# Attention stage of a hybrid encoder layer: three splits queued at other places

## The chip, the cores and the metric

One core of one Trainium2 chip runs the whole program. The metric is the time of one execution in microseconds (us) on the device; lower is better. Where several executions are compared, the median is used.

## What is computed

The program is one layer of a streaming encoder on 512 tokens of width 1024 (fp32): a token mixer with three parallel branches (trailing-mean pooling, multi-head latent attention, a spatial-gating unit), each gated and merged, then a gated feed-forward block with a short causal convolution. Only the attention branch matters here. Cut to that:

```python
q  = einsum('bsr,rhd->bshd', rms_norm(cq, g_q),  w_uq)      # 8 heads, 128 plain + 64 rotary
kv = einsum('bsr,rhd->bshd', rms_norm(ckv, g_kv), w_ukv)    # 128 key + 128 value
q_rope = rope(q[..., 128:]);  k_rope = rope(kr)             # one rotary key for all heads
for i in range(4):                                          # blocks of 128 queries
    s = q_nope @ k_nope.T + q_rope @ k_rope.T               # keys up to the end of block i
    s = where(chunk(k) <= chunk(q), s * scale, -big)        # chunks of 64
    o[i] = softmax(s) @ v
```

The key projection is folded into the query side: for each head the query and key weights are multiplied once (`attention_weights`), and scores are taken against the latent `ckv` itself.

## The kernel before, in words

Matrix products that need full fp32 accuracy are made from three products of a faster type: each operand is split into a high part, a rounded copy, and a low part, the difference. A split is one instruction on ScalarE (high) and one on VectorE (low); out of PSUM it is `split_ps` (L128 to L131), for weights out of SBUF `wsplit` (L90 to L100). `mm3` (L108) issues the three products; `mm_chunk` (L113) issues 24 products over all eight blocks of the model width, as for a gate.

The attention stage is the loop over heads at L864 to L890. Iteration h does the following:

- rows 1 to 3 of head h's scores (`score_rows`, L754): products into a PSUM tile `sc`, a memset of the masked corner (L772), the row maximum (L774), the exponential on ScalarE (L781), and the division on GpSimd (L785);
- `attend(h - 1)` (L831): the products of the transposed weights with the values, into `po`, in three groups j = 0, 1, 2 that read PTh and PTl of that j;
- `project(h + 1)` (L734): six products of head h+1's folded weights with the latent queries, into `pqn`, and the split of the result;
- in iterations 0, 2 and 4, `rotary` (L659): products for the rotary queries of the next pair of heads, a multiplication by tables on VectorE and an addition on GpSimd that leaves the tile `qtA`, and `rotary_split` (L675), which splits `qtA` into two heads' `qrT` (two half-height instructions on ScalarE, two on VectorE);
- a `gate` (L385): 24 products that depend on nothing in attention, and a tanh `th` on ScalarE (L391);
- behind the gate, `attend_last(h - 1)` (L844), which adds the last two products to `po` and splits it into `o..h` and `o..l` (needed only long after the loop); `attention_weights(h + 2)` (L714), four products into `pwm`, split into `wqk..h` and `wqk..l`, which `project` of the next iteration reads;
- row 0 of head h+1's scores, and `transposes(h)` (L809): ten transposes on TensorE into three PSUM tiles `ptp`, each split into PTh (ScalarE) and PTl (VectorE), and a copy of one block into the head's `full` tile (L828).

All PSUM tiles come from one pool of eight buffers (`ps`, L63); a tile keeps its buffer until its last reader is done. The transposed weights, the `full` tiles and `qtA` and `qtB` come from a pool of eight SBUF buffers (`pt_t`, L75).

The source order isn't the order on the engines. When the program is built, a planner with a time model fills each engine's queue: of the instructions that can run it prefers those that stand earlier in the source, and it passes over those that still wait. So work of a later head may stand ahead of work of an earlier one, and the whole program is planned anew at each build. `tc.issue_after(ins)` ties what is traced inside it behind `ins` on the queue of its own engine; it adds no wait between engines. `on_tensor` (L436) uses it to keep one line of TensorE's work in the source's order.

Of the kernel before, what the change touches and what calls it, by code (L numbers as in the profile page):

```python
# [12 lines left out]
ALU = mybir.AluOpType  # L13
# [7 lines left out]
H = 8  # L21
# [30 lines left out]
def trunk(ctx: ExitStack, tc: tile.TileContext, A, out):  # L52
    nc = tc.nc
# [12 lines left out]
    def act_t(name, dt=F32R):  # L66
        return sb.tile([P, 512], dt, name=name, tag="act", bufs=48)
# [13 lines left out]
    def f(ap):  # L81
        return ap.bitcast(F32)
# [44 lines left out]

    def split_ps(src, hi, lo, col=None):  # L128
        if col is None:
            nc.scalar.copy(out=hi, in_=src)  # L130
            nc.vector.tensor_tensor(out=lo, in0=src, in1=f(hi), op=ALU.subtract)  # L131
        else:
            nc.scalar.activation(hi, src, AF.Copy, scale=col)
            nc.vector.scalar_tensor_tensor(
                out=lo, in0=src, scalar=col, in1=f(hi), op0=ALU.mult, op1=ALU.subtract
            )
# [28 lines left out]
    for t in range(TT):  # L165
        for n in range(2):
            x_load = nc.sync.dma_start(
                out=xs[t][n], in_=A["x"][t, n]
# [267 lines left out]
    def on_tensor(work, *args):  # L436
        with ExitStack() as order:
            for ins in tensor_last:
                order.enter_context(tc.issue_after(ins))
            tensor_last[:] = [work(*args).ins]  # L440
# [138 lines left out]
    for t in range(TT):  # L579
# [3 lines left out]
        src = lat[t][:, 384:448].rearrange("p (a b) -> p a b", a=2)  # L583
        for dst, tab in ((tA, cosT), (tB, sinT)):
            nc.vector.tensor_tensor(
                out=dst[:, t, :].rearrange("p (a b) -> p a b", a=2), in0=src,
                in1=tab[:, t : t + 1, :].broadcast_to([P, 2, 32]), op=ALU.mult,
# [71 lines left out]
    def rotary(p):  # L659
        pq = ps("pq")  # L660
        c = slice(p * P, (p + 1) * P)
        for k in range(2):
            wh, wl = wqr[k]
            mm3(pq, wh[:, c], wl[:, c], cT_hi[k], cT_lo[k], k == 0, k == 1)
        tA = pt_t("qtA")
        tB = pt_t("qtB")
        nc.vector.tensor_tensor(out=tA, in0=pq, in1=turns[0], op=ALU.mult)
        for j in range(4):
            o = slice(32 * j, 32 * j + 32)
            i = slice(32 * (j ^ 1), 32 * (j ^ 1) + 32)  # L670
            nc.vector.tensor_tensor(out=tB[o, :], in0=pq[i, :], in1=turns[1][o, :], op=ALU.mult)
        nc.gpsimd.tensor_tensor(out=tA, in0=tA, in1=tB, op=ALU.add)
        return tA

    def rotary_split(p, tA):  # L675
        for h in range(2):
            q = act_t(f"qrT{2 * p + h}")
            hi = slice(64 * h, 64 * h + 64)
            lo = slice(64 - 64 * h, 128 - 64 * h)
            nc.scalar.copy(out=q[hi, :], in_=tA[hi, :])  # L680
            nc.vector.tensor_tensor(out=q[lo, :], in0=tA[hi, :], in1=f(q[hi, :]), op=ALU.subtract)
            qrT.append(q)
# [31 lines left out]
    def attention_weights(h):  # L714
        raw = const.tile([P, 384], F32, name=f"wqk{h}", tag="wqk")
        with tc.issue_after(last_load[0]):
            nc.sync.dma_start(out=raw, in_=A["wqk"][h])
        pw = ps("pwm")

        def products():  # L720
            for k in range(2):
                c = slice(k * P, (k + 1) * P)
                ins = nc.tensor.matmul(pw[:, c], raw[:, c], raw[:, 256:384], start=True, stop=True)
            return ins

        on_tensor(products)
        wh = act_t(f"wqk{h}h")[:, :256]
        wl = act_t(f"wqk{h}l")[:, :256]
        split_ps(pw[:, :256], wh, wl)
        wqk[h] = wh, wl  # L730
# [23 lines left out]
    def score_rows(h, i):  # L754
        kh, kl = cT_hi[2], cT_lo[2]
        if i == 0:
            PE_[h] = []
            whole[h] = qk[h][2]
        qh, ql, full = qk[h] if i < TT - 1 else qk.pop(h)
        qs = slice(i * P, (i + 1) * P)  # L760
        nk = (i + 1) * P
        sc = ps("sc")
        if i == 0:
            on_tensor(first_scores, sc, h, full)
        else:
            with tc.issue_after(tensor_last[0]):
                nc.tensor.matmul(sc[:, :nk], qh[:, qs], kl[:, :nk], start=True, stop=False)
            nc.tensor.matmul(sc[:, :nk], ql[:, qs], kh[:, :nk], start=False, stop=False)
            nc.tensor.matmul(sc[:, :nk], qrT[h][:, qs], krL[:, :nk], start=False, stop=False)
            nc.tensor.matmul(sc[:, :nk], qrT[h][:, qs], krT[:, :nk], start=False, stop=False)  # L770
            nc.tensor.matmul(sc[:, :nk], qh[:, qs], kh[:, :nk], start=False, stop=True)
        nc.vector.memset(sc[0:64, nk - 64 : nk], MASKED)  # L772
        mx = sm.tile([P, 4], F32, name="mx", tag="mx")
        nc.vector.reduce_max(out=mx[:, 0:1], in_=sc[:, :nk], axis=AX.X, negate=True)  # L774
        if i == 1:
            pe = first_rows_of.pop(h)[:, P:]
        else:
            pe = pad_t("pe")
        if i == 0:
            first_rows_of[h] = pe  # L780
        nc.scalar.activation(  # L781
            pe[:, :nk], sc[:, :nk], AF.Exp, bias=mx[:, 0:1], scale=1.0, accum_out=mx[:, 2:3]
        )
        nc.vector.reciprocal(out=mx[:, 3:4], in_=mx[:, 2:3])  # L784
        nc.gpsimd.tensor_scalar(  # L785
            out=pe[:, :nk], in0=pe[:, :nk], scalar1=mx[:, 3:4], scalar2=0.0, op0=ALU.mult, op1=ALU.add
        )
        if h == 0:
            PE_[h].append(pe)
        elif i == 0:  # L790
            pair[h] = pe
        else:
            pr = act_t(f"pr{h}{i}")
            if i == 1:
                nc.sync.dma_start(out=f(pr)[:, : 3 * P], in_=pair.pop(h)[:, : 3 * P])
                PE_[h] += [pr, pr[:, P:]]
            else:
                nc.sync.dma_start(out=f(pr)[:, :nk], in_=pe[:, :nk])
                PE_[h].append(pr)
# [9 lines left out]
    def transposes(h):  # L809
        pes = PE_.pop(h)  # L810
        full = whole[h]
        hs = [pt_t(f"PTh{h}{j}", F32R) for j in range(3)]
        ls = [pt_t(f"PTl{h}{j}", F32R) for j in range(3)]
        for j in range(3):
            pt = ps("ptp")

            def turn():
                for i in range(j, TT):
                    ins = flip(pt[:, (i - j) * P : (i - j + 1) * P], pes[i][:, j * P : (j + 1) * P])
                if j == 2:  # L820
                    ins = flip(pt[:, 384:512], pes[3][:, 384:512])
                return ins

            on_tensor(turn)
            b = 512 - j * P
            split_ps(pt[:, :b], hs[j][:, :b], ls[j][:, :b])
            if j == 2:
                nc.scalar.copy(out=full[:, 256:384], in_=pt[:, 384:512])  # L828
        PT[h] = hs, ls

    def attend(h):  # L831
        hs, ls = PT.pop(h)
# [11 lines left out]
    def attend_last(h):  # L844
        po, v, pt = opened.pop(h)
        on_tensor(lambda: nc.tensor.matmul(po[:, 384:512], v, pt, start=False, stop=True))
        oh = act_t(f"o{h}h")
        ol = act_t(f"o{h}l")
        split_ps(po, oh, ol)
        oT_hi.append(oh)  # L850
        oT_lo.append(ol)

    th1 = []
    tensor_last.clear()
    attention_weights(0)
    rotary_split(0, rotary(0))
    th0.append(gate(0, 3, None, gate_weights[3]))
    project(0)
# [1 line left out]
    th0.append(gate(0, 4))  # L860
    values(0, (2, 3))
    attention_weights(1)
    score_rows(0, 0)
    for h in range(H):  # L864
        for i in range(1, TT):
            score_rows(h, i)
        if h:
            attend(h - 1)
        if h == 4:
            values(1)  # L870
        if h == 0:
            turned = rotary(1)
        if h + 1 < H:
            project(h + 1)
        if h in (2, 4):
            rotary_split(h // 2 + 1, rotary(h // 2 + 1))
        if len(th0) < KT:
            th0.append(gate(0, len(th0)))
        elif len(th1) < 5:
            th1.append(gate(1, len(th1)))  # L880
        with tc.issue_after(last_chunk[0]):
            if h:
                attend_last(h - 1)
            if h + 2 < H:
                attention_weights(h + 2)
        if h == 0:
            rotary_split(1, turned)
        if h + 1 < H:
            score_rows(h + 1, 0)
        transposes(h)  # L890


    ada_state = {}
# [145 lines left out]
    pool(1)  # L1039
    attend(H - 1)  # L1040
    attend_last(H - 1)
    for m in range(KT):
        if m and m + 1 < KT:
            pool(m + 1)
        merge(0, m, oT_hi, oT_lo, th0[m])
        behind_split(ada_piece, 0, m)
        if m == 6:
            behind_split(combine_weights, 0)
# [952 lines left out]
```

## Time and profile before

| what | value |
|---|---|
| median of 3 runs | 928.01 us (927.05 to 928.98) |
| the profiled execution's own time | 926.81 us |
| its span, first to last instruction | 925.1 us |
| around the span | 1.7 us |
| TensorE busy over the span | 911.8 us, 4388 products |
| VectorE, ScalarE, GpSimd busy | 669.9, 408.0, 259.0 us |
| mean granted TensorE clock | 0.997 of full |
| attention loop in the trace | about 74 to 182 us |

A row of a timeline has the start in us from the span's start, the time it took, the engine, the line, the operation, `out<-in` by the program's names with the buffer numbers left out, shapes, and in brackets how long the engine was idle before it and what ended that. PE is TensorE, PEld its weight loads, DVE VectorE, ACT ScalarE, POOL GpSimd. Product ends are modelled and overlap the next start, so starts tell more than durations. A row of windows has a stretch, its length, the busy time and number of instructions of PE, PEld, DVE, ACT and POOL, the granted clock, and the DMA engines' share and rate.

### The profile page before, as it was taken

The page shows a single profiled execution, that of the slowest core. Times are in us where ns is not written, and L with a number is a line of the kernel's source. Part 1 is how long each engine was busy: PE and PEld are TensorE (multiplying, and loading weights), DVE is VectorE, ACT ScalarE, POOL GpSimd, SP SyncE. Part 2 cuts the span into 40 slices and gives each one's busy share as a digit, 9 for nine tenths or more (in the row PEclk, how much of TensorE's full clock was granted, in tenths as well). Part 3 has the DMA queues.
Part 4 walks back from the last instruction along what each step waited for, and adds up shares of the span by engine and source line. Part 5 has one row for each costly group of instructions (what it writes and reads, how often), then busy time and mean ns, then how long its engine had stood idle before and what let it go on. Part 6 is the DMA issues. An engine that isn't in the chain of part 4 may idle for free. (4 is left out here: it accounts for less than half of the span.)

```text
span 925.1 us, 12529 instructions
## 1 busy us (share of the span) xinstructions
PE 911.8 (99%) x4388; PEld 768.5 (83%) x4388; DVE 669.9 (72%) x1094; ACT 408.0 (44%) x676; POOL 259.0 (28%) x314
## 2 busy tenths in 40 slices
PE   7999999999999999999999999999999999999996
PEld 6888888888888888888888888988888888888885
DVE  7977566447777798776475589588888766676787
ACT  5676555532333332133322346464554555455421
POOL 4621211113431154402053711032223221120304
PEclk9999999999999999999999999999999999999998
DMA  9832333245447986774476450045554553479946
GB/s 356 304 115 76 101 110 105 91 148 166 157 145 263 376 322 223 249 257 144 158 263 216 144 195 27 23 150 189 189 179 129 154 174 126 137 272 357 348 137 159
DMA packets 70959, 171.94 MB, mean 186 GB/s; under 512 B 9312, under 2 KB 12576, under 8 KB 70896
## 3 DMA queue, kind: packets, MB, share of 16 engines
q1 hardware_dynamic: 58752, 142.14, 45.6%
q0 software_dynamic: 11712, 28.51, 9.1%
q8 instruction: 34, 0.56, 0.2%
q10 hardware_dynamic: 432, 0.49, 0.1%
q14 instruction: 29, 0.24, 0.1%
HBM read 144.16 MB, written 20.78 MB: 178 GB/s over the span
## 5 line engine op out<-in xcount | busy, mean ns | idle before, releaser
L96 DVE TENSOR_TENSOR wupl<-wup,wuph 128x1024 fp32r<-128x1024 f32 x38 | 52.4, 1378 | 25.1 <-PE pzu L122 17.0
L1659 POOL TENSOR_TENSOR zc<-zc 128x512 f32<-128x512 f32 x22 | 31.2, 1420 | 130.3 <-ACT zc L1658 128.9
L95 ACT CAST wuph<-wup 128x1024 fp32r<-128x1024 f32 x38 | 40.1, 1054 | 46.4 <-PE pzu L120 31.1
L95 ACT CAST wbh<-wb 128x1024 fp32r<-128x1024 f32 x24 | 25.3, 1054 | 68.2 <-PE py L120 44.2
L96 DVE TENSOR_TENSOR wgl<-wg,wgh 128x1024 fp32r<-128x1024 f32 x22 | 28.8, 1307 | 31.6 <-PE pg L122 17.7
L1034 POOL DMA_DIRECT2D wt<-wb x44 | 24.2, 551 | 80.1 <-DVE wb L1030 75.1
L1635 ACT ACTIVATE zc<-pzu,cols 128x512 f32<-128x512 f32 x44 | 34.0, 778 | 21.0 <-PE pzu L122 16.6
L95 ACT CAST wgh<-wg 128x1024 fp32r<-128x1024 f32 x22 | 23.2, 1055 | 40.7 <-PE pg L120 29.7
L905 DVE SCALAR_TENSOR_TENSOR ada<-adar,cact,ada 128x512 f32<-128x512 f32 x42 | 40.6, 1004 | 0.5 <-DMA adar<-in_ada 0.5
L1030 DVE TENSOR_TENSOR wb<-wb,wb 128x512 f32<-128x512 f32 x44 | 35.3, 806 | 6.8 <-DMA wb<-in_wdn 6.4
L785 POOL TENSOR_SCALAR pe<-pe,mx 128x128 f32<-128x128 f32 (+3 forms) x32 | 17.0, 534 | 76.6 <-DVE mx L784 56.6
L96 DVE TENSOR_TENSOR wbl<-wb,wbh 128x1024 fp32r<-128x1024 f32 x24 | 31.1, 1297 | 9.8 <-PE pg L122 5.3
L1638 DVE SCALAR_TENSOR_TENSOR zc<-pzu,cols,zc 128x511 f32<-128x511 f32 x44 | 32.5, 742 | 4.3 <-ACT zc L1635 4.3
L1642 DVE SCALAR_TENSOR_TENSOR zc<-pzu,cols,zc 128x510 f32<-128x510 f32 x44 | 32.6, 744 | 0.7
L409 POOL TENSOR_TENSOR mg<-mg,th 128x512 f32<-128x512 f32 x16 | 28.4, 1778 | 11.6 <-DVE th L406 11.4
L986 POOL TENSOR_TENSOR asum<-apad 128x527 f32<-128x527 f32 x8 | 12.2, 1520 | 59.1 <-issue 30.0
L1699 POOL DMA_DIRECT2D z<-ys x27 | 14.5, 541 | 49.2 <-PE pd L1675 39.4
L1658 ACT ACTIVATE zc<-zc 128x512 f32<-128x512 f32 x22 | 13.9, 631 | 20.9 <-DVE zc L1642 20.9
L96 DVE TENSOR_TENSOR wal<-wa,wah 128x1024 fp32r<-128x1024 f32 x8 | 10.7, 1333 | 17.1 <-PE pg L122 9.9
L1210 POOL TENSOR_TENSOR oraw<-oraw,gtt 128x512 f32<-128x512 f32 x6 | 10.3, 1729 | 39.7 <-DMA oraw<-in_wo 37.4
L781 ACT ACTIVATE pe<-sc,mx 128x128 f32<-128x128 f32 (+3 forms) x32 | 16.9, 529 | 10.1 <-DVE mx L774 7.6
L1232 POOL TENSOR_TENSOR o<-o,gtt 128x512 f32<-128x512 f32 x10 | 17.5, 1773 | 12.6 <-DMA o<-in_wo 10.2
(1627 smaller groups left out, 3204.4 us busy)
## 6 DMA issues: line engine op xcount, KB each, us to landing
wup<-in_wup SPq DMA_DIRECT2D x44, 512.0 KB, 3.5
wb<-in_wb SPq DMA_DIRECT2D x24, 512.0 KB, 3.8
adar<-in_ada SPq DMA_DIRECT2D x48, 256.0 KB, 4.9
wg<-in_wg SPq DMA_DIRECT2D x23, 512.0 KB, 3.6
wb<-in_wdn SPq DMA_DIRECT2D x44, 256.0 KB, 5.3
wt<-wb POOLq DMA_DIRECT2D x44, 256.0 KB, 4.2
ada<-in_ada SPq DMA_DIRECT2D x32, 256.0 KB, 5.3
z<-ys POOLq DMA_DIRECT2D x27, 256.0 KB, 5.7
```

The costliest lines, as they stand in the source:

```text
L95: nc.scalar.copy(out=hi[:, :n], in_=raw[:, :n])
L96: ins = nc.vector.tensor_tensor(out=lo[:, :n], in0=raw[:, :n], in1=f(hi[:, :n]), op=ALU.subtract)
L409: nc.gpsimd.tensor_tensor(out=merged[m], in0=merged[m], in1=th, op=ALU.add)
L785: nc.gpsimd.tensor_scalar(out=pe[:, :nk], in0=pe[:, :nk], scalar1=mx[:, 3:4], scalar2=0.0, op0=ALU.mult, op1=ALU.add)
L905: nc.vector.scalar_tensor_tensor(out=acc[n], in0=src, scalar=cact[:, k : k + 1], in1=acc[n], op0=ALU.mult, op1=ALU.add,)
L1030: ins = nc.vector.tensor_tensor(out=dst, in0=x, in1=y, op=op)
L1034: nc.gpsimd.dma_start(out=dst, in_=src)
L1232: nc.gpsimd.tensor_tensor(out=halves[n], in0=halves[n], in1=gt[n], op=ALU.mult)
L1635: nc.scalar.activation(t, pz, AF.Identity, bias=cols[:, cc + 3 : cc + 4], scale=cols[:, cc + 2 : cc + 3])
L1638: nc.vector.scalar_tensor_tensor(out=t[:, 1:512], in0=pz[:, 0:511], scalar=cols[:, cc + 1 : cc + 2], in1=t[:, 1:512], op0=ALU.mult, op1=AL ...
L1642: nc.vector.scalar_tensor_tensor(out=t[:, 2:512], in0=pz[:, 0:510], scalar=cols[:, cc : cc + 1], in1=t[:, 2:512], op0=ALU.mult, op1=ALU.add,)
L1659: nc.gpsimd.tensor_tensor(out=val, in0=val, in1=gate, op=ALU.mult)
```

## The change

Three things are queued elsewhere. The split of the folded query/key weights leaves `attention_weights` and becomes `attention_weights_split`; the split of each head's output leaves `attend_last` and becomes `attended_split`. In the loop both are now traced after `transposes(h)`, and tied behind its last split (j = 2): on ScalarE behind the last PTh, on VectorE behind the last PTl. `rotary_split` is now traced one iteration after its `rotary`, after the next `project`. The first two heads' weights and the last head's output are split at once, as before.

```diff
     def split_ps(src, hi, lo, col=None):
         if col is None:
-            nc.scalar.copy(out=hi, in_=src)
-            nc.vector.tensor_tensor(out=lo, in0=src, in1=f(hi), op=ALU.subtract)
+            a = nc.scalar.copy(out=hi, in_=src)
+            b = nc.vector.tensor_tensor(out=lo, in0=src, in1=f(hi), op=ALU.subtract)
+            return a.ins, b.ins
...
         on_tensor(products)
+        wqk[h] = pw
+
+    def attention_weights_split(h):
+        pw = wqk[h]
         wh = act_t(f"wqk{h}h")[:, :256]
         wl = act_t(f"wqk{h}l")[:, :256]
         split_ps(pw[:, :256], wh, wl)
...
-            split_ps(pt[:, :b], hs[j][:, :b], ls[j][:, :b])
+            turned_split = split_ps(pt[:, :b], hs[j][:, :b], ls[j][:, :b])
             if j == 2:
                 nc.scalar.copy(out=full[:, 256:384], in_=pt[:, 384:512])
         PT[h] = hs, ls
+        return turned_split
...
         on_tensor(lambda: nc.tensor.matmul(po[:, 384:512], v, pt, start=False, stop=True))
+        opened[h] = po
+
+    def attended_split(h):
+        po = opened.pop(h)
         oh = act_t(f"o{h}h")
         ol = act_t(f"o{h}l")
         split_ps(po, oh, ol)
...
     attention_weights(0)
+    attention_weights_split(0)
...
     attention_weights(1)
+    attention_weights_split(1)
...
         if h + 1 < H:
             project(h + 1)
+        if h in (1, 3, 5):
+            rotary_split((h + 1) // 2, turned)
         if h in (2, 4):
-            rotary_split(h // 2 + 1, rotary(h // 2 + 1))
+            turned = rotary(h // 2 + 1)
...
-        if h == 0:
-            rotary_split(1, turned)
         if h + 1 < H:
             score_rows(h + 1, 0)
-        transposes(h)
+        with ExitStack() as behind:
+            for ins in transposes(h):
+                behind.enter_context(tc.issue_after(ins))
+            if h + 2 < H:
+                attention_weights_split(h + 2)
+            if h:
+                attended_split(h - 1)
...
     attend_last(H - 1)
+    attended_split(H - 1)
```

## The prediction

> **What bounds the kernel now.** I read the page's first part, then its busy time in windows cut at the same point of each attention head (from one head's query/key weight products to the next's), then the timeline of TensorE where a window was longer than its neighbours, then VectorE and ScalarE beside it.
>
> The page's engine line:
>
> ```profile
> PE 911.8 (99%) x4388; PEld 768.5 (83%) x4388; DVE 669.9 (72%) x1094; ACT 408.0 (44%) x676; POOL 259.0 (28%) x314
> ```
>
> TensorE (PE) is the bound. So an edit that leaves its work alone, as this one does, can only win what PE loses in stalls. Busy time in windows, for heads 1, 3, 5 and 6:
>
> ```profile
> 84.80:98.30 13.50, 13.46 (x75) 11.57 (x74) 7.65 (x20) 7.84 (x20) 2.19 (x5) 1.00 0.33 104
> 112.70:126.00 13.30, 13.21 (x76) 11.41 (x75) 7.62 (x21) 7.49 (x19) 2.14 (x4) 1.00 0.31 105
> 143.10:156.90 13.80, 13.51 (x75) 11.31 (x74) 8.13 (x21) 7.98 (x19) 2.74 (x5) 1.00 0.29 100
> 156.90:169.90 13.00, 13.00 (x75) 11.45 (x75) 6.63 (x19) 7.33 (x19) 2.13 (x4) 1.00 0.26 92
> ```
>
> Columns: stretch, length, then busy time of PE, weight loads, VectorE, ScalarE and GpSimd, and TensorE's granted clock. Head 6 does a like number of products in 13.00 us without a stall; heads 1, 3 and 5 take 0.50, 0.30 and 0.80 us more, while VectorE and ScalarE are busy for hardly half the time. What is lost is lost by order, not by load. (Some of head 1's excess is not a stall: its window holds head 0's transposes, which are done in another type.)
>
> The stalls themselves, TensorE's timeline in heads 1, 3 and 5:
>
> ```profile
> 89.38 0.39 PE L770 MATMUL sc<-krT,qrT 128*128 128x512 f32 x1
> 89.60 0.40 PE L771 MATMUL sc<-cT2h,q1h 128*128 128x512 f32 x1
> 90.04 0.47 PE L109 MATMUL po<-PTl,V00h 128*128 128x512 f32 x1
> 90.34 0.40 PE L110 MATMUL po<-PTh,V00l 128*128 128x512 f32 x1
> ```
> ```profile
> 116.00 0.33 PE L770 MATMUL sc<-krT,qrT 128*128 128x384 f32 x1
> 116.17 0.34 PE L771 MATMUL sc<-cT2h,q3h 128*128 128x384 f32 x1
> 116.60 0.47 PE L767 MATMUL sc<-cT2l,q3h 128*128 128x512 f32 x1
> 116.90 0.39 PE L768 MATMUL sc<-cT2h,q3l 128*128 128x512 f32 x1
> ```
> ```profile
> 146.59 0.34 PE L771 MATMUL sc<-cT2h,q5h 128*128 128x384 f32 x1
> 147.12 0.50 PE L767 MATMUL sc<-cT2l,q5h 128*128 128x512 f32 x1 [0.20 <-ACT pe L781]
> 147.47 0.40 PE L768 MATMUL sc<-cT2h,q5l 128*128 128x512 f32 x1
> ...
> 148.17 0.40 PE L771 MATMUL sc<-cT2h,q5h 128*128 128x512 f32 x1
> 148.67 0.47 PE L109 MATMUL po<-PTl,V10h 128*128 128x512 f32 x1
> 148.97 0.40 PE L110 MATMUL po<-PTh,V10l 128*128 128x512 f32 x1
> ```
>
> Read the starts, not the durations: a product overlaps its neighbour, so a late start hardly shows as idle time. An undisturbed 512-column product is followed after 0.22 to 0.23 us (89.38 to 89.60), a 384-column one after 0.17 (116.00 to 116.17). Over that, with the slow restart behind each stall: head 1 loses 0.21 + 0.07 us, head 3 0.26 + 0.07, head 5 0.36 + 0.12 and 0.27 + 0.07. In all **1.43 us**. There are two kinds. A score row's last 512 columns (116.60, 147.12) wait for a PSUM buffer: there are eight, and the one that comes free is that of the head's row 0, when its exponential has read it. The first product of `attend` (90.04, 148.67) waits for the low half of the first transposed weights (PTl).
>
> On the engine line the Trainium skill (Perfetto Trace Analysis, Identifying the Most-Contended Engine) says that TensorE's busy share misleads, and that headroom is judged by the share of weight loads. The windows agree in part. PE's gaps in the three windows are 0.42 us by busy time, 1.43 by starts. Brought to head 6's weight-load share (11.45 of 13.00, 88%) they would lose 0.35 + 0.33 + 0.95 = 1.6 us. By that page's measure the ceiling would be 1.6 us; but head 6 has 88% with no stall at all, so the page's other 83% is no reserve. I use 1.43.
>
> **The change part by part.** No instruction is added or removed and no DMA moves; the weights' load stays with its products. What changes is the order on ScalarE and VectorE. VectorE in head 3, then in head 5, then ScalarE in head 5:
>
> ```profile
> 114.72 0.69 DVE L681 TENSOR_TENSOR qrT<-qtA,qrT 64x512 fp32r<-64x512 f32 x1
> 115.44 0.29 DVE L774 TENSOR_REDUCE mx<-sc 128x1 f32<-128x128 f32 x1
> 115.76 0.69 DVE L131 TENSOR_TENSOR o1l<-po,o1h 128x512 fp32r<-128x512 f32 x1
> ...
> 116.48 0.67 DVE L131 TENSOR_TENSOR PTl<-ptp,PTh 128x512 fp32r<-128x512 f32 x1
> 117.07 0.40 DVE L131 TENSOR_TENSOR wqk4l<-pwm,wqk4h 128x256 fp32r<-128x256 f32 x1
> ```
> ```profile
> 145.34 1.40 DVE L681 TENSOR_TENSOR qrT<-qtA,qrT 64x512 fp32r<-64x512 f32 x2
> ...
> 146.90 0.69 DVE L131 TENSOR_TENSOR o3l<-po,o3h 128x512 fp32r<-128x512 f32 x1
> ...
> 147.84 0.68 DVE L131 TENSOR_TENSOR PTl<-ptp,PTh 128x512 fp32r<-128x512 f32 x1
> ```
> ```profile
> 145.52 0.58 ACT L130 CAST o3h<-po 128x512 fp32r<-128x512 f32 x1
> 145.98 0.60 ACT L130 CAST PTh<-ptp 128x512 fp32r<-128x512 f32 x1
> ```
>
> *Output split behind the transposed splits.* In head 5 PTl waits behind o3l (0.69 us) on VectorE. Without it PTl ends near 148.52 - 0.69 = 147.8, while attend, with row 3 on time, would want it at 148.67 - 0.27 - 0.36 - 0.12 = 147.9: that stall goes. On ScalarE o3h leaves the way of PTh, and the exponential behind PTh comes some 0.5 us earlier: that about pays the 0.36 + 0.12. Head 3 gains 0.69 us for PTl as well, but its stall is row 3's, and row 0's maximum (115.44), which its exponential needs, stands behind a rotary low half and not behind o1l. So head 3's 0.33 goes only if the rotary split moves too. Head 1 has no output to split (its stall falls in iteration 0's transposes); there the weights' split (0.40 us, as wqk4l) leaves the way, more than the 0.28 lost.
>
> *Rotary split later.* 0.69 us for each VectorE half, two to a pair of heads. It is due only one head later, and head 6's window leaves VectorE idle for 13.00 - 6.63 us, which hides it at no cost; if that cover were gone it would cost up to its own 1.4 us on VectorE, once for each of three pairs. But it can't be put off as far as the source says. The pool that holds its source (`pt`, 8 buffers) must at that point also hold two heads' `full` tiles and the six transposed tiles, nine in all; so the sixth, the last PTl, must wait until both rotary halves have been read. Between PTl's first and last is where I expect them. I give head 3 half of its 0.33: **0.17**.
>
> *Weights' split last.* Here the change can lose. It now ends after the last PTl on VectorE, and the next `project` (pqn) reads it. Head 6, as an undisturbed example, VectorE and PE:
>
> ```profile
> 159.41 0.41 DVE L131 TENSOR_TENSOR wqk7l<-pwm,wqk7h 128x256 fp32r<-128x256 f32 x1
> 159.74 0.68 DVE L131 TENSOR_TENSOR PTl<-ptp,PTh 128x512 fp32r<-128x512 f32 x1
> ...
> 161.37 0.40 DVE L131 TENSOR_TENSOR PTl<-ptp,PTh 128x256 fp32r<-128x256 f32 x1
> ```
> ```profile
> 160.61 0.39 PE L767 MATMUL sc<-cT2l,q6h 128*128 128x512 f32 x1
> ...
> 162.69 0.39 PE L110 MATMUL pqn<-cT0h,wqk7l 128*128 128x512 f32 x1
> ```
>
> After the change the same VectorE work stands ahead of wqk7l's end, less the output's split, so it ends by 161.77 at the latest; it is wanted at 162.69. 0.9 us of slack: heads 2, 4, 6 and 7 lose nothing. In heads 1 and 5 the two rotary halves (1.40) are in the same stretch. In head 5 the first PTl would end near 147.8; behind it come row 1's maximum, two PTl and the weights (0.4 to 0.5 each), about 149.6 with them in a row; pqn's second product would want it at 147.9 + 4 x 0.23 = 148.8. The bounds are 0 (the planner puts attend's next three products, 3 x 0.17, and more of the gate in front) and about 0.8 us a head in two heads. I take **0.25 us in all**, near the lower bound, because the order is planned with such waits in view and there are the gate's products to fill with.
>
> Sum: head 1 0.28, head 5 0.82, head 3 0.17, less 0.25: **1.0 us**. Behind attention PE has no wait that this would meet, and the gain is carried to the end. The profiled execution took 926.81 us, so 925.8 by its own measure; it lies below the median of the three runs, 928.01, from which the forecast is **927.0**. The case's own bounds: head 3 regains 0 to 0.33, the project's wait takes 0 to 0.7 (more is the next case), so 0.4 to 1.4 us of gain, 926.6 to 927.6.
>
> **The rivals.**
>
> *Nothing to measure either way.* The project's wait takes the place of the ones removed: 2 x 0.8 lost against 1.27 to 1.43 gained, 0.2 to 0.3 slower or, with half of it, 0.5 faster: 927.5 to 928.3, say 928.0. For it: in every transition pqn directly follows attend's first three products. Against it: the planner has other work.
>
> *Slower: PSUM.* `po` and `pwm` now hold two of eight buffers until behind the last PTl, some 2 us longer in each transition. In head 6 row 3 takes its buffer at 160.61. The first PTl, freed of the weights' split ahead of it, ends about 160.42 - 0.41 = 160.0 and gives one back, 0.6 us before. If that slipped by more than 0.6 us, row 3 would stall in heads 2, 4, 6 and 7 as it does now in head 5 (0.48), and heads 1, 3, 5 would keep theirs: 4 x 0.48 = 1.9, so 929.9. Against it stands that the splits ahead of PTl are just what is taken away.
>
> *Slower: the clock.* Shorter, more frequent pauses could lower the granted clock. Head 5 paused for 0.36 and 0.27 us and its granted clock stayed at 1.00. If the four windows' 53.6 us fell to 0.9 of it, that is 6 us: 934. The Trainium skill (TensorE: Matmul & The Clock Gate, A second HAM failure mode: psum-queue depth-cycling) says that cycling through PSUM banks can make TensorE pause often enough for its clock to swing; the 1.00 beside these pauses speaks against it here.
>
> *More than the stalls.* A new plan takes also the short restarts at other places, or better orders the stages behind: over 1.9 us, about 926.0. Nothing in the rows asks for it, but the order of the whole program is planned anew at each build.
>
> **How the numbers follow.** Forecast 0.57, nothing either way 0.23, PSUM 0.09, clock 0.01, more 0.10. The measurement of this kernel can tell about 0.2% (1.9 us; the three runs before spread over as much). Faster by that: all of the last case and 0.07 of the forecast, where scatter adds: 0.17. Slower: PSUM and clock, less what scatter hides, 0.09. The same: 0.74. The range must leave out no more than 2 in 10: it takes both middle cases with a microsecond of scatter and most of "more": 925.7 to 928.9.
>
> **What would show it.** In the profile after: windows of heads 1 and 5 near 13.0 to 13.2 us; no late start at row 3 or at attend's first product; PTl ahead of o-low and wqk-low on VectorE; rotary halves ahead of the last PTl. Wrong would be: pqn starting over 0.3 us late behind wqk-low in heads 1, 3 or 5 (the project's wait), row 3 waiting in an even head (PSUM), a window's clock under 1.00, or a difference that arises behind 182 us.

## The result, and the profile after

Fourteen runs of each kernel (those before include the three of the table before the change): 925.84 us after (925.11 to 926.11), 927.12 us before (926.73 to 928.98). The ratio is 0.9984, with a 95% interval of 0.9977 to 0.9992: about 1.5 us faster, between 0.7 and 2.1; the medians differ by 1.28. It is small, but clear of the noise. Beside the later experiments, before had medians of 926.90 to 927.01. The profiled execution after took 925.74 us, with a span of 924.0.

The windows of heads 1, 3, 5 and 6 after the change, with the columns of before:

```profile
85.00:98.40 13.40, 13.40 (x75) 11.75 (x74) 6.54 (x19) 7.40 (x19) 2.28 (x5) 1.00 0.32 105
112.70:125.80 13.10, 13.10 (x76) 11.52 (x75) 7.11 (x20) 7.65 (x19) 3.23 (x5) 1.00 0.33 107
142.80:155.80 13.00, 13.00 (x76) 11.42 (x74) 7.34 (x21) 7.53 (x19) 4.48 (x5) 1.00 0.33 107
155.80:168.80 13.00, 13.00 (x76) 11.49 (x75) 8.05 (x21) 7.62 (x20) 2.15 (x4) 1.00 0.26 92
```

Head 5 lost its 0.80 us of excess and head 3 its 0.30 but for a rounding; head 1 was 0.50 over head 6 and is 0.40, with windows cut to a tenth; its late start is gone from the starts, and what is left I had put down to the other type of head 0's transposes, which no run separates. The prediction started from the median of three runs before, 928.01; that of fourteen is 927.12, so 0.89 of the 1.16 us between the forecast and the measured time lie in that start. No window has idle time left. TensorE in head 5:

```profile
146.26 0.33 PE L776 MATMUL sc<-cT2h,q5h 128*128 128x384 f32 x1
146.43 0.39 PE L772 MATMUL sc<-cT2l,q5h 128*128 128x512 f32 x1
...
147.35 0.39 PE L776 MATMUL sc<-cT2h,q5h 128*128 128x512 f32 x1
147.58 0.40 PE L109 MATMUL po<-PTl,V10h 128*128 128x512 f32 x1
...
148.28 0.34 PE L109 MATMUL po<-PTl,V11h 128*128 128x384 f32 x1
...
148.81 0.40 PE L109 MATMUL pqn<-cT0l,wqk6h 128*128 128x512 f32 x1
149.05 0.39 PE L119 MATMUL pg<-hT0l,wgh 128*128 128x512 f32 x1
```

Row 3 of the scores starts 0.17 us after row 2's last product, and attend's first product 0.23 us after row 3's: both late starts are gone. What follows is new. The planner puts attend's group j = 1 (148.28) ahead of project, issues project's first product (148.81), and goes on with the gate (149.05); project's second product, which reads wqk-low, starts only at 153.05. VectorE at the same time:

```profile
145.27 0.69 DVE L131 TENSOR_TENSOR PTl<-ptp,PTh 128x512 fp32r<-128x512 f32 x1 [0.29 <-ACT PTh L130]
...
146.06 0.53 DVE L131 TENSOR_TENSOR PTl<-ptp,PTh 128x384 fp32r<-128x384 f32 x1
...
148.02 0.42 DVE L131 TENSOR_TENSOR PTl<-ptp,PTh 128x256 fp32r<-128x256 f32 x1
148.36 0.41 DVE L131 TENSOR_TENSOR wqk6l<-pwm,wqk6h 128x256 fp32r<-128x256 f32 x1
```

The first PTl ends at 145.96, 3.2 us into the head's window (from 142.8); before it ended at 148.52, 5.4 us into its own (from 143.1). The third starts only at 148.02, just after attend's first product (147.58, 0.40 us) has read the first; and wqk-low stands behind it and ends at 148.77. With project right behind attend's first group (at 148.28) the second product would have been due at about 148.51, ahead of that; at 149.04, behind group j = 1, it would have found wqk-low ready. That the gate comes next all the same is the planner's choice, and costs nothing. The rotary halves, meanwhile, are far away, at the end of the next head:

```profile
155.76 0.69 DVE L682 TENSOR_TENSOR qrT<-qtA,qrT 64x512 fp32r<-64x512 f32 x1
156.48 1.23 DVE L96 TENSOR_TENSOR wgl<-wg,wgh 128x1024 fp32r<-128x1024 f32 x1
157.74 0.69 DVE L682 TENSOR_TENSOR qrT<-qtA,qrT 64x512 fp32r<-64x512 f32 x1
```

One measure serves for all runs below, and I call it **the stretch**: from the start of the first weight product of head 2 (before, at 85.22) to the start of the last product of head 6's `attend_last` (before, at 181.46, as the timeline of the products into `po` has them). Before it is 96.23 us, after 94.79: 1.44 us shorter, against the 1.43 that the late starts had added up to. In this execution the stretch began 0.26 us later than in the one before, which is why the spans differ by only 1.1; from the stretch's end to the span's end it is 743.6 us before and 743.7 after.

### The profile page after: what moved, and what is told of

Its sections match the earlier page's. It is cut to its first block, busy times and chain, and to the rows that moved or that the text cites. A ratio compares the mean times of both kernels' runs of the same rounds, so it can differ in the third digit from the quotient of the medians.

```text
span 924.0 us, 12535 instructions
## 1 busy us (share of the span) xinstructions
PE 910.7 (99%) x4388; PEld 768.6 (83%) x4388; DVE 669.3 (72%) x1094; ACT 408.2 (44%) x676; POOL 260.1 (28%) x314
```

## Experiments

| kernel | median us | before beside it | ratio (95%) | stretch us |
|---|---|---|---|---|
| before | | | | 96.23 |
| the change | 925.84 | 927.12 | 0.9984 (0.9977 to 0.9992) | 94.79 |
| rotary part alone | 925.97 | 926.96 | 0.9988 (0.9979 to 0.9997) | 94.86 |
| output and weights parts alone | 927.03 | 926.96 | 0.9999 (0.9990 to 1.0008) | 96.18 |
| output part alone | 927.38 | 926.90 | 1.0005 (0.9996 to 1.0014) | 96.50 |
| extra work in even heads | 926.14 | 926.90 | 0.9990 (0.9981 to 0.9999) | 94.86 |
| the same, placed first | 927.92 | 927.01 | 1.0010 (1.0001 to 1.0018) | 97.01 |
| tanh ahead of the rotary casts | 926.66 | 927.01 | 0.9995 (0.9986 to 1.0003) | 95.81 |
| rotary split behind, same head | 925.83 | 927.01 | 0.9986 (0.9977 to 0.9995) | 94.86 |
| change, seven PSUM buffers | 929.02 | 926.96 | 1.0022 (1.0013 to 1.0031) | 98.26 |
| rotary part, seven buffers | 926.02 | 926.90 | 0.9990 (0.9981 to 0.9999) | 94.95 |
| change, project first | 927.28 | 926.96 | 1.0003 (0.9994 to 1.0012) | 96.06 |
| the same, nine `pt` buffers | 925.66 | 926.90 | 0.9990 (0.9981 to 0.9999) | 94.70 |

**The rotary part alone.** Against the change: the output and weights splits go back to where they were.

```diff
             if h:
                 attend_last(h - 1)
+                attended_split(h - 1)
             if h + 2 < H:
                 attention_weights(h + 2)
+                attention_weights_split(h + 2)
...
-        with ExitStack() as behind:
-            for ins in transposes(h):
-                behind.enter_context(tc.issue_after(ins))
-            if h + 2 < H:
-                attention_weights_split(h + 2)
-            if h:
-                attended_split(h - 1)
+        transposes(h)
```

> Only the rotary split is queued one iteration later; outputs and weights are split where they were before. Theory (output and weights splits stood in the way of the transposed weights): the rotary part alone frees head 3's row 0 maximum, so it wins 0.17 to 0.33 us, and head 5's and head 1's stalls stay at about half or more: 0.3 to 0.7 us faster than before in all. Rival (rotary split alone was in the way): the three stalls stand in exactly the heads that follow a rotary split, and heads 2, 4 and 6, with the same output and weights splits, have none; then all 1.43 us go with this part alone.

The stretch is 94.86 us, 1.37 shorter than before: all three late starts are gone with this part alone. My theory fell and the rival stood. TensorE in head 5 of this kernel, with row 3 and attend on time:

```profile
146.22 0.33 PE L776 MATMUL sc<-cT2h,q5h 128*128 128x384 f32 x1
146.40 0.39 PE L772 MATMUL sc<-cT2l,q5h 128*128 128x512 f32 x1
...
147.32 0.39 PE L776 MATMUL sc<-cT2h,q5h 128*128 128x512 f32 x1
147.55 0.40 PE L109 MATMUL po<-PTl,V10h 128*128 128x512 f32 x1
```

**The output and weights parts alone.** Against the change: the rotary calls of before.

```diff
-        if h in (1, 3, 5):
-            rotary_split((h + 1) // 2, turned)
         if h in (2, 4):
-            turned = rotary(h // 2 + 1)
+            rotary_split(h // 2 + 1, rotary(h // 2 + 1))
...
+        if h == 0:
+            rotary_split(1, turned)
```

> Only the output and weights splits go behind the transposed weights; the rotary split stays where it was before. Theory: heads 1 and 5 regain 0.28 + 0.82 us, head 3 keeps up to 0.33: 1.1 us faster than before. Rival (rotary alone was in the way): the rotary halves still stand ahead of the first PTl, so at most 0.3 us is won.

Nothing is won in all (96.18 us), but not because nothing changed. Head 1's late start is gone, as the prediction had it for the weights' split; TensorE there:

```profile
90.06 0.39 PE L776 MATMUL sc<-cT2h,q1h 128*128 128x512 f32 x1
90.29 0.40 PE L109 MATMUL po<-PTl,V00h 128*128 128x512 f32 x1
```

What head 1 wins, head 3 loses: its stall has moved. TensorE, then ScalarE, in head 3 of this kernel:

```profile
115.54 0.28 PE L776 MATMUL sc<-cT2h,q3h 128*128 128x256 f32 x1
115.96 0.44 PE L772 MATMUL sc<-cT2l,q3h 128*128 128x384 f32 x1
```
```profile
114.02 1.26 ACT L681 CAST qrT<-qtA 64x512 fp32r<-64x512 f32 x2 [1.93 <-POOL qtA L673]
115.31 0.60 ACT L392 ACTIVATE th<-pg 128x512 f32<-128x512 f32 x1
115.80 0.58 ACT L130 CAST PTh<-ptp 128x512 fp32r<-128x512 f32 x1
```

Now already row 2 starts late (0.42 us after a 256-column product). With `po` and `pwm` held, it needs the gate's own PSUM buffer, which the tanh (115.31) gives back; and the tanh stands behind rotary casts that waited 1.93 us for GpSimd.

**The output part alone.** Against the kernel above: the weights' split goes back too, and only `attended_split` follows the transposes.

```diff
             if h + 2 < H:
                 attention_weights(h + 2)
+                attention_weights_split(h + 2)
...
         with ExitStack() as behind:
             for ins in transposes(h):
                 behind.enter_context(tc.issue_after(ins))
-            if h + 2 < H:
-                attention_weights_split(h + 2)
             if h:
                 attended_split(h - 1)
```

> Only the output's split goes behind the transposed weights; weights and rotary queries are split where they were before. My prediction gave this part head 5's 0.82 us and half a head 3. Theory now (each of the two late splits takes a PSUM buffer from the scores, and with the rotary split still in front the gain on VectorE is paid back in a wait for a buffer): 0 to 0.5 us faster than before, a late start at row 2 or row 3 in heads 3 and 5 still in the trace. Rival (my prediction): 0.8 to 1 us faster, no late start in head 5.

No gain: 1.0005, and the stretch is 0.27 us longer than before, outside the 0 to 0.5 us faster that I had expected. This is the part to which I had given the whole of head 5. TensorE there:

```profile
146.84 0.34 PE L776 MATMUL sc<-cT2h,q5h 128*128 128x384 f32 x1
147.82 0.47 PE L772 MATMUL sc<-cT2l,q5h 128*128 128x512 f32 x1 [0.64 <-DVE wqk6l L131]
```

Row 3 now starts 0.8 us later than its 0.17, and the buffer that it gets is `pwm`'s, given back by wqk-low, which VectorE takes only behind both rotary halves. In head 3 there is no late start at row 3. The heads one by one, in us from the head's first weight product to the next head's:

| kernel | head 1 | head 3 | head 5 |
|---|---|---|---|
| before | 13.51 | 13.31 | 13.85 |
| the change | 13.27 | 13.04 | 13.04 |
| rotary part alone | 13.25 | 13.03 | 13.03 |
| output and weights parts alone | 13.27 | 13.53 | 13.85 |
| output part alone | 13.48 | 13.09 | 14.33 |

So the late weights' split is enough for head 1 and the late output split for most of head 3, with the rotary split still in front; head 5 is freed by neither (the weights' split was not moved alone), and with both moved head 3 stalls again. Only the rotary part frees all three. Each of these programs was planned anew, so the queues differ in more than the part that was moved.

**Extra work in even heads.** To see whether the rotary halves hurt by their load, the rotary part alone, with the like of a rotary split put into the transitions to heads 2, 4 and 6 (VectorE's half of it, against the rotary part alone):

```diff
+        if i == 0 and h in (2, 4, 6):
...
+            for g in range(2):
...
+                with tc.issue_after(ins):
+                    ins = nc.vector.tensor_tensor(
+                        out=extra[down, :], in0=turns[0][up, :], in1=f(extra[up, :]), op=ALU.subtract
+                    ).ins
+            maximum_after.enter_context(tc.issue_after(ins))
```

> The kernel with the rotary part alone (no stall left), and in the transitions into heads 2, 4 and 6 work of the size and place of a rotary split: two half-height copies of a table on ScalarE, early, and two half-height differences on VectorE queued between row 0's memset and its maximum. Nobody reads what they leave; the output is the same. Theory now (two half-height differences, 1.4 us on VectorE, ahead of row 0's maximum or of PTl are what makes TensorE stall): heads 2, 4 and 6 now lose 0.3 to 1 us each as heads 1, 3 and 5 did, 0.9 to 3 us slower than the rotary part alone. Rival (VectorE has room there, and the stalls came from something else in those heads, such as the late addition on GpSimd): under 0.3 us.

The stretch stays at 94.86 us: 1.4 us more on VectorE in each of three transitions cost nothing that shows. The theory as I held it then fell too. VectorE in the transition to head 2 shows where the two halves came to lie:

```profile
100.29 0.67 DVE L131 TENSOR_TENSOR o0l<-po,o0h 128x512 fp32r<-128x512 f32 x1
100.99 0.69 DVE L786 TENSOR_TENSOR extra<-cosR,extra 64x512 fp32r<-64x512 f32 x1
101.70 0.42 DVE L131 TENSOR_TENSOR wqk3l<-pwm,wqk3h 128x256 fp32r<-128x256 f32 x1
102.05 0.68 DVE L131 TENSOR_TENSOR PTl<-ptp,PTh 128x512 fp32r<-128x512 f32 x1
...
102.87 0.69 DVE L786 TENSOR_TENSOR extra<-cosR,extra 64x512 fp32r<-64x512 f32 x1
```

Row 0's maximum comes only after 103.4, so its PSUM buffer is far too late for row 3. But the output's split stands first, and has given `po`'s buffer back by 100.96. In heads 3 and 5 of the kernel before, the order was the other way round: rotary halves, then output.

**The same, placed first.** Against the run above, the splits of these transitions are tied behind the two extra halves. (In all transitions the output's and weights' splits are also traced behind row 0 of the scores.)

```diff
-                attended_split(h - 1)
...
-                attention_weights_split(h + 2)
...
-        transposes(h)
+        with tc.issue_after(extra_last[0]) if h in (1, 3, 5) else ExitStack():
+            if h:
+                attended_split(h - 1)
+            if h + 2 < H:
+                attention_weights_split(h + 2)
+            transposes(h)
```

> As the run with extra work in heads 2, 4 and 6, but on VectorE the row maximum, the output's and the weights' split and the transposed splits of these transitions are tied behind the two extra halves, as they stood behind the rotary halves in heads 3 and 5 of the kernel before. (Output unchanged.) Refined theory (not the load but the place: while the rotary halves stand ahead of the output's split and of the row maximum, no PSUM buffer comes free for row 3, and the first PTl is late): a late start at row 3 or at attend in each of the three heads, 0.3 to 1 us each, 0.9 to 3 us slower than the rotary part alone. Rival (VectorE's order does not matter either; it was GpSimd's late addition): no late start, within 0.3 us.

2.15 us more in the stretch, and 927.92 us. VectorE and TensorE in the same transition:

```profile
99.88 1.41 DVE L786 TENSOR_TENSOR extra<-cosR,extra 64x512 fp32r<-64x512 f32 x2
101.20 0.28 DVE L793 TENSOR_REDUCE mx<-sc 128x1 f32<-128x128 f32 x1
101.52 0.69 DVE L131 TENSOR_TENSOR o0l<-po,o0h 128x512 fp32r<-128x512 f32 x1
```
```profile
101.54 0.34 PE L777 MATMUL sc<-cT2h,q2h 128*128 128x384 f32 x1
102.35 0.47 PE L773 MATMUL sc<-cT2l,q2h 128*128 128x512 f32 x1 [0.48 <-DVE o0l L131]
```

Same instructions, other order: row 3 starts 0.64 us late and waits, by name, for the output's low half. This repeats at will, in heads that had no stall, what head 3 had before: there the output's low half ended at 116.45 (115.76, 0.69 us), 0.15 us ahead of row 3's start at 116.60; here it ends at 102.21, 0.14 ahead of 102.35. In these heads it is the buffer of `po`, not time on VectorE, that was short. Head 5 before was not the same: there the output's low half came later still (it ended at 147.59), and row 3 (147.12) took row 0's buffer, as its line names. VectorE, then ScalarE, in head 5 before:

```profile
145.02 0.29 DVE L774 TENSOR_REDUCE mx<-sc 128x1 f32<-128x128 f32 x1
```
```profile
143.74 1.26 ACT L680 CAST qrT<-qtA 64x512 fp32r<-64x512 f32 x2 [0.94 <-POOL qtA L672]
145.02 0.60 ACT L391 ACTIVATE th<-pg 128x512 f32<-128x512 f32 x1
...
146.61 0.37 ACT L781 ACTIVATE pe<-sc,mx 128x128 f32<-128x128 f32 x1
```

Row 0's maximum was ready at 145.31, ahead of the rotary halves (145.34). Its exponential came at 146.61, behind rotary casts that had waited 0.94 us for GpSimd, the tanh, and the two casts that the prediction shows. So row 3 was late in head 5 by ScalarE's queue, which the next run tests.

**Tanh ahead of the rotary casts.** The kernel before, with one tie on ScalarE; for it the rotary split of iterations 2 and 4 is also traced behind the gate.

```diff
-        nc.scalar.activation(th, pg, AF.Tanh, scale=0.5)
+        ins = nc.scalar.activation(th, pg, AF.Tanh, scale=0.5)
+        last_tanh[:] = [ins.ins]
...
-        if h in (2, 4):
-            rotary_split(h // 2 + 1, rotary(h // 2 + 1))
+        if h in (2, 4):
+            turned = rotary(h // 2 + 1)
...
+        if h in (2, 4):
+            with tc.issue_after(last_tanh[0]):
+                rotary_split(h // 2 + 1, turned)
```

> The kernel before, with the rotary casts of iterations 2 and 4 tied behind the gate's tanh on ScalarE, so that ScalarE no longer waits for GpSimd's addition with the tanh queued behind it; nothing else moves. Theory (two causes: ScalarE held up by that wait in head 5, VectorE's order in heads 1 and 3): head 5 loses less than 0.4 us instead of 0.82, heads 1 and 3 keep their 0.28 and 0.33 or a little more: 0.2 to 0.6 us faster than before. Rival (place on VectorE alone): no change, or slower by up to 0.5 us, since the casts now stand ahead of the output's split.

The stretch is 0.42 us shorter; the time, 0.9995 with an interval that includes no change, agrees but can't show it by itself. ScalarE, then TensorE, in head 5:

```profile
143.48 0.60 ACT L391 ACTIVATE th<-pg 128x512 f32<-128x512 f32 x1 [0.72 <-PE pg L122]
143.98 1.25 ACT L682 CAST qrT<-qtA 64x512 fp32r<-64x512 f32 x2
...
146.35 0.37 ACT L783 ACTIVATE pe<-sc,mx 128x128 f32<-128x128 f32 x1
```
```profile
146.56 0.34 PE L773 MATMUL sc<-cT2h,q5h 128*128 128x384 f32 x1
146.86 0.50 PE L769 MATMUL sc<-cT2l,q5h 128*128 128x512 f32 x1
```

Head 5's late starts (by starts, as in the prediction) fall from 0.82 to 0.48 us: a little over the 0.4 that I had set. Row 3 now comes 0.30 us after row 2's last product instead of 0.53. So about 0.3 us of head 5 was ScalarE's wait for GpSimd's addition with the tanh and the output's cast queued behind it. The remaining 0.5 goes when the rotary split leaves the transition; how it divides between the rotary casts on ScalarE and the halves on VectorE no run shows.

**Rotary split behind, same head.** The rotary split stays in its own iteration, tied behind the last transposed split; output and weights are split early. Against the rotary part alone:

```diff
-        if h in (1, 3, 5):
-            rotary_split((h + 1) // 2, turned)
...
-        transposes(h)
+        with ExitStack() as behind:
+            for ins in transposes(h):
+                behind.enter_context(tc.issue_after(ins))
+            if h in (0, 2, 4):
+                rotary_split(h // 2 + 1, turned)
```

> The kernel before, with the rotary split of each pair kept in its own iteration but tied behind the last transposed split; output and weights are split where they were. Theory (it is enough that the rotary split is out of the transition's way; one head later is only one way to get there): the stalls of heads 1, 3 and 5 go, 1 to 1.4 us faster than before, like the rotary part alone. Rival (in the same head it still delays row maxima and the query's split): 0.5 us faster or less.

94.86 us and 0.9986: one head later is only one way; out of the transition is what counts.

**Seven PSUM buffers.** An unused tile holds one of the eight through the loop, once in the change, once in the rotary part alone.

```diff
+    held = ps("held")
+    nc.vector.memset(held[:, 0:8], 0.0)
     for h in range(H):
...
+        nc.vector.tensor_copy(out=freed, in_=held[:, 0:8])
```

> The changed kernel with one of the eight PSUM buffers held by an unused tile from before the loop over heads to behind it (one 8-column memset and one 8-column copy more). Theory (the eight buffers leave some 0.6 us of slack although po and pwm are held longer): with seven, row 3 or already row 2 of the scores waits for a buffer in each of seven heads, 0.3 to 1 us a head, 2 to 7 us slower than the changed kernel. Rival (buffers are not short at all): no stall, within 0.3 us of the changed kernel.

> The rotary part alone, with one PSUM buffer held by an unused tile as in the seven-buffer run of the changed kernel. Theory (po and pwm, held behind the last PTl, are what used up the slack): with both given back early, seven buffers do: no stall or under 0.3 us a head, within 1 us of the rotary part alone, at least 1.5 us faster than the changed kernel with seven. Rival (seven are too few whoever holds them): the same 3 us lost.

The change with seven: stretch 3.47 us longer, 929.02 us, with late starts in five heads (2 to 6) rather than in the seven that I had expected. TensorE in head 2, where the first PTl has not yet given back its buffer when row 2 wants one:

```profile
101.23 0.28 PE L776 MATMUL sc<-cT2h,q2h 128*128 128x256 f32 x1
102.07 0.44 PE L772 MATMUL sc<-cT2l,q2h 128*128 128x384 f32 x1 [0.56 <-DVE PTl L131]
```

The rotary part alone with seven: 94.95 us, as good as with eight. So the late output and weights splits do cost PSUM buffers; with eight, and no rotary split in front, there are enough, but not one to spare.

**Project first.** The change, with everything that TensorE could put ahead of project's products tied behind them; then the same with nine buffers in the `pt` pool (and 47 instead of 48 in the large pool; the last two lines are this second run's).

```diff
         if h:
-            attend(h - 1)
+            attend(h - 1, (0,))
         if h + 1 < H:
             project(h + 1)
+        with tc.issue_after(projected[0]):
+            if h:
+                attend(h - 1, (1, 2))
...
-        return sb.tile([P, 512], dt, name=name, tag="pt", bufs=8)
+        return sb.tile([P, 512], dt, name=name, tag="pt", bufs=9)
```

> The changed kernel, with attend's groups j = 1 and 2, the values, the rotary products and the gate tied on TensorE behind the six products of project, so that nothing can be put in front of them. Theory (the project's wait was priced at 0 because the planner fills it, not because there is none): project's second product waits for wqk-low, 0.3 to 0.6 us in each of heads 1 to 6, 1.8 to 3.6 us slower than the changed kernel, 0.3 to 2 us slower than the kernel before. Rival (wqk-low is early enough by itself): within 0.5 us of the changed kernel.

> The run in which nothing may be put in front of project's products, with nine instead of eight buffers in the pool of the transposed tiles (and 47 instead of 48 in the large pool, to make room). Theory (in heads 1, 3 and 5 the sixth transposed tile is the ninth in the pool and takes the first PTl's buffer only when attend's first product has read it; the weights' split stands behind it): with nine the 0.43 us stalls at project's second product go, about 1.3 us faster than with eight. Rival (VectorE is simply late there): the stalls stay.

With eight, the stretch is 1.27 us longer than the change's. TensorE in head 3:

```profile
118.61 0.40 PE L109 MATMUL pqn<-cT0l,wqk4h 128*128 128x512 f32 x1
119.16 0.50 PE L110 MATMUL pqn<-cT0h,wqk4l 128*128 128x512 f32 x1 [0.15 <-DVE wqk4l L131]
```

A wait of 0.32 us and a slow restart, but in heads 1, 3 and 5 alone; I had expected all six, 1.8 to 3.6 us. Those three are the heads where `qtA` is still held. With nine buffers, the same two products and the third PTl:

```profile
121.47 0.39 PE L109 MATMUL pqn<-cT0l,wqk4h 128*128 128x512 f32 x1
121.70 0.39 PE L110 MATMUL pqn<-cT0h,wqk4l 128*128 128x512 f32 x1
```
```profile
120.09 0.40 DVE L131 TENSOR_TENSOR PTl<-ptp,PTh 128x256 fp32r<-128x256 f32 x1
120.42 0.40 DVE L131 TENSOR_TENSOR wqk4l<-pwm,wqk4h 128x256 fp32r<-128x256 f32 x1
```

No wait, and the stretch is 94.70 us. So the wait was for the ninth tile's buffer. (In this profiled execution, 928.96 us, the loop began over 3 us later than in the others, which the stretch leaves out; that kernel's median is 925.66.)

None of these versions is faster than the change by what can be measured: every one without late starts has a stretch of 94.7 to 95.0 us.

## Why the prediction was right and wrong

**What bounds, and what there was to win: right.** TensorE's starts gave 1.43 us as all that an edit of order could win; the stretch lost 1.44, and none of those late starts is left. The share of weight loads also came to 88% in heads 1, 3 and 5 (11.75 of 13.40, 11.52 of 13.10, 11.42 of 13.00), head 6's share before. My estimate by that share, the measure of the Trainium skill (Perfetto Trace Analysis, Identifying the Most-Contended Engine), had put the ceiling at 1.6 us; the measured 1.44 lies 0.2 us below it.

**The sum: its two discounts were wrong.** I took off 0.25 us for project's wait and gave head 3 only half of its 0.33. The first came out at 0, the second at the whole 0.33: 1.4 instead of 1.0 us. Where nothing may be put in front, project's second product does wait for wqk-low (0.32 us in heads 1, 3 and 5); in the change the planner put attend's next group and the gate in front, which I had named as the lower bound and should have taken. The larger miss of the forecast time, 0.89 of 1.16 us, was none of the mechanism: the three runs before had a median of 928.01, fourteen have 927.12.

**The chances: wrong.** I put 0.74 on a change too small to measure, with 0.2% as what can be told. Fourteen runs of each kernel told 0.16% with an interval of 0.08% to either side. The step that failed here is "the measurement of this kernel can tell about 0.2% (1.9 us; the three runs before spread over as much)": the spread of single runs isn't the uncertainty of a median of many. With 0.08% (0.7 us) as what can be told, "faster" was the likeliest outcome of my own sum of 1.0 us.

**The part by part cost: wrong, and the deepest error.** The step that failed in the mechanism is the price of each part. I gave head 5's 0.82 us to the output's split and head 1's 0.28 to the weights', because they stood ahead of the waiting PTl, and only half of head 3's 0.33 to the rotary split. The runs give all three to the rotary split, which alone wins 1.37 of the 1.44 us. Head 1's price for the weights' split was right as far as it went: that split moved late frees head 1 too. Head 5's was wrong: with the output's split alone moved, head 5 takes 0.48 us more, not 0.82 less. Head 3's reading was wrong in the buffer: row 3 waited there for `po`'s, given back by the output's low half, 0.15 us ahead, and not for row 0's, which the exponential had read by 116.28; with the output's split alone moved, row 3 comes on time there, the rotary split still in front. That the sum came near was luck: the change holds all the parts, so it did not matter to which of them I gave a stall. The rows held the warning: heads 2, 4 and 6 had the same output and weights splits ahead of PTl, and no stall. The one thing that heads 1, 3 and 5 had of their own was the rotary split. I also counted only what stood in PTl's way, and not that the output's split, by standing early, hands row 3 its buffer.

**The rotary split's limit: wrong.** I had written that "the sixth, the last PTl, must wait until both rotary halves have been read". Nine tiles for eight buffers was right, and project first with nine buffers shows that it binds. But the buffer that comes free first is the first PTl's, which attend's first product alone reads; the halves went a head later, as the source says.

**The rivals.** PSUM did not decide, with eight buffers; in the parts alone and with seven it did: row 2 or row 3 waited for a buffer, as the rival described. The slack that I had put at 0.6 us in even heads wasn't measured in microseconds, but it is less than one buffer. The clock stayed at 1.00 in the windows shown. Nothing arose behind the loop (743.6 and 743.7 us from the stretch's end to the span's).

## What to carry to other kernels

Where some rounds of a loop stall and others don't, look first for what only the stalled ones contain; the instruction just ahead of the late one in the queue may be innocent, or only one of several whose move would do. An evacuation that nobody needs for a long time still gives back a PSUM buffer, so deferring it isn't free: test with one buffer less to see how much room is left. And the same work on an engine that has idle time can cost nothing or two microseconds, by its place in the queue alone. A total that comes out doesn't show that its terms were right; the parts run one by one do.

## What the runs showed of the hardware that was not expected

A late start costs more than the wait: behind each in the kernel before, the next product comes 0.07 to 0.12 us later than its usual 0.23. And TensorE's idle time shows little of it: 0.42 us in the three windows before, against 1.43 by starts, since a product's record (0.39 us) outlasts its turn (0.23).
